# Moving the streamed matmul operands of a four-layer block kernel to one fixed distance from the weights in SBUF

## The chip, the core and the metric

One NeuronCore of a Trainium2 chip runs the whole program in one launch. The metric is the device time of one execution in microseconds. The kernel before takes 1949.94 us (median of 3 runs, 1945.63 to 1951.67).

## What is computed

Two stacked blocks of depth 2 each, in float32, on 256 tokens of width 1024. The first block's layer is a gated MLP, a mixer of three branches (a gated linear recurrence, latent attention, a long depthwise convolution) and a second gated MLP; the second block's layer is an attention mixer and a gated MLP with a short convolution.

```python
def first_block(x, ...):
    for l in range(DEPTH):                       # 2
        x = x + 0.5 * swiglu(rms_norm(x, ffn1_norm[l]), ffn1_w1[l], ffn1_w2[l])
        x = x + hybrid_mixer(rms_norm(x, mix_norm[l]), ...)
        x = x + 0.5 * swiglu(rms_norm(x, ffn2_norm[l]), ffn2_w1[l], ffn2_w2[l])
    return rms_norm(x, final_norm)

def second_block(x, ...):
    for l in range(DEPTH):                       # 2
        x = x + rms_norm_2(hybrid_mixer_2(rms_norm_2(x, attn_pre_norm[l]), ...), attn_post_norm[l])
        x = x + rms_norm_2(conv_ffn(rms_norm_2(x, ffn_pre_norm[l]), ...), ffn_post_norm[l])
    return x
```

The MLPs are 1024 to 2 x 2816 to 1024. Nearly all of the arithmetic is in products of activations with weight matrices that are read once from HBM.

## The kernel before

**One product, three matmuls.** Every weight slab and every activation is held as two `float32r` tiles, a rounded part h and a remainder l. `mm3` (L226 to L229) forms w.x as wh.xh + wh.xl + wl.xh, three matmuls that accumulate in one PSUM bank. In each, a 128 x 128 part of the weights is the stationary operand, which the PE loads with a LDWEIGHTS, and a 128 x 256 slice of the activations (all 256 tokens) is streamed past it. Each matmul thus has a weight load of its own, and the profile shows the loads (engine PEld) beside the matmul of the part before. `tokens3` (L265 to L272) does the same with the roles exchanged: weights are streamed, 256 or 512 columns at a time, past a 128 x 128 part of the activations.

**Slabs.** `Slab` (L186 to L207) brings 128 x 1024 weights (512 KB) by one SyncE DMA (L183) into one of four `raw` tiles; ScalarE copies them to `wh`, VectorE subtracts to `wl` (both L198). A slab feeds 24 matmuls of `mm3`. The tiles rotate through 6 buffers of the pool `w`; in the second block every seventh slab uses a seventh pair of buffers in the pool `w2`, which lies where the first block's scratch was.

**Streamed tiles.** `xh`, `xl` (pool `act`, L508) are the normalised input of every projection; `hh`, `hl` (L591) the hidden layer of the MLPs (pool `ffn`); `r0` to `r3` (pool `mix1`, L694) the branch outputs of the first mixer; `mxh`, `mxl` (pool `mix2`, L1140) the heads' outputs in the second. They are allocated by stack pools in the order in which the program opens them, so each one's address follows from what was opened before it.

**Stages.** Up projections of the MLPs: 11 x 4 groups of 24 matmuls, 1056 in all, with `xh`/`xl` streamed; there are six. Down projections: 528 matmuls with `hh`/`hl` streamed, five times; the sixth and last (L1295) streams the weights 512 wide. The mixers hold the other projections, the attention heads (plain float32 matmuls, L651 to L666) and, on VectorE, a convolution of 31 taps (L916). PE runs in program order; DVE and ACT run the splits of coming slabs and the work behind each projection in the order that the framework fixed. All instruction orders are the same before and after the change.

**Where the tiles lie.** A slab's rows are 512 or 1024 bytes apart, the streamed rows 1024 bytes, so the distance between the start of what is streamed and the start of the weights that are loaded meanwhile, modulo 512 bytes, is one number for each pair of pools. The program's allocation gives, in bytes of a partition modulo 512:

| streamed tile | its start | distance to weights in `w` (start 320) | to weights in `w2` (start 128) |
|---|---|---|---|
| `xh`, `xl` | 320 | 0 | 192 |
| `hh`, `hl` | 128 | 320 | 0 |
| `r0` to `r3` | 160 | 352 | not used together |
| `mxh`, `mxl` | 416 | 96 | 288 |

Where weights are streamed (`tokens3`), the distance is that of the weights to the loaded activations: 0 for `xh`, and 192 (pool `w`) or 0 (pool `w2`) for `hh`. Below, "distance" means this number. SBUF is used to byte 229,152 of 229,376 in each partition, 16,384 of them as scratch for dynamic DMAs.

Of the kernel before, what the change touches and what calls it, by code (L numbers as in the profile page):

```python
# [7 lines left out]
F32 = mybir.dt.float32  # L8
# [8 lines left out]
P = 128  # L17
# [123 lines left out]
def kernel(ctx: ExitStack, tc: tile.TileContext, p, out: bass.AP):  # L141
    nc = tc.nc
# [3 lines left out]
    wpools = [ctx.enter_context(tc.tile_pool(name="w", bufs=6))]  # L146
    act = ctx.enter_context(tc.tile_pool(name="act", bufs=1))
    tmp = ctx.enter_context(tc.tile_pool(name="tmp", bufs=2))
    pso = ctx.enter_context(tc.tile_pool(name="pso", bufs=1, space=PSUM))
    banks = {}  # L150

    @contextmanager
    def psums(n):

        if banks.get('n') == n:
            yield
            return
        with ExitStack() as st:
            banks['n'] = n
            banks['lin'] = st.enter_context(tc.tile_pool(name="psl", bufs=n, space=PSUM, reuse_waits="tile"))  # L160
            if n == 4:
                banks['att'] = st.enter_context(tc.tile_pool(name="psa", bufs=1, space=PSUM, reuse_waits="tile"))
            yield
            banks['n'] = 0
# [439 lines left out]
    def ffn1(w1, w2, cur, nxt, mid=None):  # L604
        with tc.tile_pool(name="ffn", bufs=1, reuse_waits="tile") as fp, psums(7):
            hid = new_hidden(fp)
            a = cur.a
            for jp, pss, r in first_pairs(a, w1, cur.done):
                for i in range(2):
                    j = jp * 2 + i  # L610
                    g = tmp.tile([P, T], F32, name="g")
                    V.tensor_tensor(g, pss[i][:, :T], r, op=ALU.mult)  # L612
                    sg_ = tmp.tile([P, T], F32, name="sg")
                    S.activation(sg_, g, AF.Silu)  # L614
                    u = tmp.tile([P, T], F32, name="u")
                    V.tensor_tensor(u, pss[2 + i][:, :T], r, op=ALU.mult)
                    V.tensor_tensor(u, u, sg_, op=ALU.mult)
                    split(hid.h[:, j, :], hid.l[:, j, :], u)
            if mid is not None:
                mid()  # L620
            project_down(w2, hid, res_add(nxt, 0.5), table=mid is None)
# [66 lines left out]
    def mixer1(l, cur, nxt):  # L688
        a = cur.a
        w = p['w_in'][l]  # L690
        mp = ctx2.enter_context(tc.tile_pool(name="mix1", bufs=1, reuse_waits="tile"))
        fs = [mp.tile([P, n], F32, name=f"f{i}") for i, n in enumerate((1280, 1280, 1036, 1024, 1024, 2048, 0, 1144, 1024)) if n]
        fs.insert(6, fs[5][:, 1024:])
        rs = [mp.tile([P, n], F32R, name=f"r{i}") for i, n in enumerate((1280, 1280, 1024, 1024))]  # L694
        v4 = lambda t_, k=4: t_[:, :k * T].rearrange("p (k n) -> p k n", k=k)
        for par in range(2):
# [254 lines left out]
    def mixer2(l, cur, post):  # L951
        a = cur.a
        w = p['w_in_2'][l]
        mp = ctx2.enter_context(tc.tile_pool(name="mix2", bufs=1, reuse_waits="tile"))
# [180 lines left out]
        for m in range(2):  # L1135
            PE.matmul(ps[:, 0:64], hvr[:, m].rearrange("p j g n -> p (j g n)"), w2s[1][:, m, :], start=m == 0, stop=m == 1)
        V.tensor_tensor(vcz.rearrange("p a i d -> p (a i) d"), ps[:, 0:64].rearrange("p (o d) -> p o d", o=1).to_broadcast([P, 8, 64]),
                        hmask[:, :, None].to_broadcast([P, 8, 64]), op=ALU.mult)

        mix = Act(mp.tile([P, 8, T], F32R, name="mxh"), mp.tile([P, 8, T], F32R, name="mxl"))  # L1140
        os = {}

# [122 lines left out]
    def ffn2(l, cur, post, fp):  # L1265
        hid = new_hidden(fp)
        a = cur.a
        wu = p['w_up_2'][l]
        ups = [fp.tile([P, T + 2], F32, name=f"up{i}") for i in range(4)]
        for u in ups:  # L1270
            G.memset(u[:, 0:2], 0.0)
        n = 0
        for jp, pss, r in first_pairs(a, wu, cur.done):
            for i in range(2):
                j = jp * 2 + i
                cs = []
                for half in range(2):
                    jj = j + KF * half
                    u = ups[n % 4]
                    n += 1  # L1280
                    V.tensor_tensor(u[:, 2:], pss[2 * half + i][:, :T], r, op=ALU.mult)
                    c = tmp.tile([P, T], F32, name="g" if half else "u")
                    S.activation(c, u[:, 0:T], AF.Identity, scale=prm('cw0', l, jj), bias=prm('cb2', l, jj))
                    for q in (1, 2):
                        V.scalar_tensor_tensor(c, u[:, q:q + T], prm('cw%d' % q, l, jj), c, op0=ALU.mult, op1=ALU.add)
                    cs.append(c)
                sg = tmp.tile([P, T], F32, name="sg")
                S.activation(sg, cs[0], AF.Silu)
                V.tensor_tensor(sg, sg, cs[1], op=ALU.mult)
                split(hid.h[:, j, :], hid.l[:, j, :], sg)  # L1290
        if post is None:
            return hid
        project_down(p['w_down_2'][l], hid, post.take)
# [67 lines left out]
    for l in range(2):  # L1361
        cur, nxt = nxt, Next('mix_norm', l)
        ffn1(p['ffn1_w1'][l], p['ffn1_w2'][l], cur, nxt, prep1 if l == 0 else None)
        if l == 0:
            start.close()
        cur, nxt = nxt, Next('ffn2_norm', l)
        with ExitStack() as ctx2:
            ctx2.enter_context(psums(4))
            mixer1(l, cur, nxt)
        cur, nxt = nxt, Next('ffn1_norm', 1) if l == 0 else Joint()  # L1370
        ffn1(p['ffn2_w1'][l], p['ffn2_w2'][l], cur, nxt)
    wpools.append(ctx.enter_context(tc.tile_pool(name="w2", bufs=1)))
    for l in range(2):
        cur = nxt
        with ExitStack() as ctx2:
            pp = ctx2.enter_context(tc.tile_pool(name="post1", bufs=1, reuse_waits="tile"))
            ctx2.enter_context(psums(4))
            post = Post(pp, 'attn_post_norm', l)
            mixer2(l, cur, post)
            nxt = Next('ffn_pre_norm', l)  # L1380
            post.done(nxt)
        cur = nxt
        with ExitStack() as ctx2:
            pp = ctx2.enter_context(tc.tile_pool(name="ffn", bufs=1, reuse_waits="tile"))
            ctx2.enter_context(psums(7))
            if l == 0:
                post = Post(pp, 'ffn_post_norm', l)
                ffn2(l, cur, post, pp)
                nxt = Next('attn_pre_norm', 1)
                post.done(nxt)  # L1390
            else:
                last(l, ffn2(l, cur, None, pp), pp)
# [21 lines left out]
```

## Time and profile before

| | |
|---|---|
| median of 3 runs | 1949.94 us |
| the profiled execution | 1949.49 us |
| its span, first to last instruction | 1947.8 us |
| PE busy | 1921.6 us (99%), 15292 matmuls |
| DVE busy | 1498.5 us (77%) |
| ACT busy | 1122.6 us (58%) |
| granted TensorE clock, mean | 0.997 |
| HBM traffic | 167 GB/s over the span |

The matmuls are pipelined: each is shown with a length of about 0.28 us, but they start about 0.12 us apart, so the pace of PE is read from the starts of successive matmuls (the timeline), not from the mean length of one. "PE busy" is the union of the overlapping lengths and says only that PE has hardly a gap. A row of a timeline gives the start in us from the span's start, the length, and the instruction; a row of stages gives, for each engine, busy time and number of instructions in that stretch.

### The profile page before, as it was taken

What the parts mean: (1) busy time and instruction counts of PE and PEld (TensorE: products, weight loads), DVE (VectorE), ACT (ScalarE), POOL (GpSimd) and SP (SyncE); (2) the same over time, 40 slices, a digit from 0 to 9 for tenths busy, and PEclk for the clock granted to TensorE, in tenths of its full rate; (3) what the DMA queues carried; (4) which work ended last, traced back from release to release, by engine and by line L of the source; (5) the groups of instructions that cost most, each with busy time, mean ns of one, the idle gap of its engine ahead of it and who ended that gap; (6) DMA issues with size and microseconds to landing.
All of it is one profiled execution on the core that took longest, in us unless ns stands there. A gap on an engine that the chain in (4) does not pass through costs nothing.

```text
span 1947.8 us, 38941 instructions
## 1 busy us (share of the span) xinstructions
PE 1921.6 (99%) x15292; PEld 1872.8 (96%) x15292; DVE 1498.5 (77%) x3041; ACT 1122.6 (58%) x1895; POOL 75.5 (4%) x225
## 2 busy tenths in 40 slices
PE   8999999999999999999999999999999999999998
PEld 8999999999999999999999999988999999899997
DVE  7667798896665665699987666877799778769983
ACT  6445677564444544568565445456667545657653
POOL 8000000000000000000000000110000011000000
PEclk9999999999999999999999999999999999999999
DMA  8655545546555555654546555571366547234652
GB/s 252 192 169 186 169 147 154 181 157 193 185 175 191 186 184 171 184 179 132 154 160 198 182 176 183 148 226 47 97 193 208 180 130 219 86 109 152 207 195 86
DMA packets 329879, 327.36 MB, mean 168 GB/s; under 512 B 16956, under 2 KB 323648, under 8 KB 329696
## 3 DMA queue, kind: packets, MB, share of 16 engines
q1 hardware_dynamic: 326336, 322.71, 53.0%
q0 software_dynamic: 3344, 2.16, 0.5%
q8 instruction: 120, 1.97, 0.4%
q14 instruction: 63, 0.52, 0.1%
q10 hardware_dynamic: 16, 0.00, 0.0%
HBM read 323.76 MB, written 1.05 MB: 167 GB/s over the span
## 4 chain that ended last, share of the span: by engine, by line
PE 87%; DVE 8%; ACT 2%; DMA 2%; issue 1%; SPq 0%; DVEq 0%; ACTq 0%
PE lin L227 25%; PE lin L229 25%; PE lin L228 25%; DVE wl L198 3%; PE o L665 2%; PE lin L270 1%; PE lin L272 1%; PE lin L271 1%; PE pt L651 1%; DMA raw<-in_w_in_dram 1%; PE sc L660 1%; DVE f L916 1%; ACT wh L198 1%; PE o L666 1%; PE sc L659 1%
## 5 line engine op out<-in xcount | busy, mean ns | idle before, releaser
L198 DVE TENSOR_TENSOR wl<-raw,wh 128x1024 fp32r<-128x1024 f32 (+2 forms) x644 | 748.7, 1168 | 306.2 <-ACT wh L198 301.7
L198 ACT CAST wh<-raw 128x1024 fp32r<-128x1024 f32 (+2 forms) x644 | 642.7, 1003 | 531.7 <-PE lin L228 371.3
L227 PE MATMUL lin<-xh,wh 128*128 128x256 f32 (+1 forms) x3120 | 884.3, 285 | 2.5 <-ACT xh L504 1.5
L228 PE MATMUL lin<-xl,wh 128*128 128x256 f32 (+1 forms) x3120 | 885.7, 284 | 0.0
L229 PE MATMUL lin<-xh,wl 128*128 128x256 f32 (+1 forms) x3120 | 884.7, 284 | 0.0
L227 PEld LDWEIGHTS lin<-xh,wh 128*128 128x128 f32 (+1 forms) x3120 | 596.6, 192 | 5.6 <-ACT xh L504 2.9
L228 PEld LDWEIGHTS lin<-xl,wh 128*128 128x128 f32 (+1 forms) x3120 | 598.6, 192 | 0.9
L229 PEld LDWEIGHTS lin<-xh,wl 128*128 128x128 f32 (+1 forms) x3120 | 598.1, 192 | 0.7
L227 PE MATMUL lin<-hh,wh 128*128 128x256 f32 x880 | 246.0, 279 | 0.0
L229 PE MATMUL lin<-hh,wl 128*128 128x256 f32 x880 | 245.5, 279 | 0.0
L228 PE MATMUL lin<-hl,wh 128*128 128x256 f32 x880 | 245.3, 279 | 0.0
L229 PEld LDWEIGHTS lin<-hh,wl 128*128 128x128 f32 x880 | 165.4, 188 | 0.0
L227 PEld LDWEIGHTS lin<-hh,wh 128*128 128x128 f32 x880 | 165.2, 188 | 0.0
L228 PEld LDWEIGHTS lin<-hl,wh 128*128 128x128 f32 x880 | 164.9, 187 | 0.0
L227 PE MATMUL lin<-r,wh 128*128 128x256 f32 x372 | 107.9, 290 | 0.5 <-ACT f L870 0.4
L229 PE MATMUL lin<-r,wl 128*128 128x256 f32 x372 | 106.7, 287 | 0.0
L228 PE MATMUL lin<-r,wh 128*128 128x256 f32 x372 | 105.7, 284 | 0.0
L916 DVE SCALAR_TENSOR_TENSOR f<-f,pcol,f 128x256 f32<-128x256 f32 x240 | 103.6, 479 | 0.9
L227 PEld LDWEIGHTS lin<-r,wh 128*128 128x128 f32 x372 | 70.1, 189 | 1.6 <-ACT f L870 0.8
L228 PEld LDWEIGHTS lin<-r,wh 128*128 128x128 f32 x372 | 70.6, 190 | 0.3
L614 ACT ACTIVATE sg<-g 128x256 f32<-128x256 f32 x88 | 35.6, 413 | 60.8 <-DVE g L612 60.7
L229 PEld LDWEIGHTS lin<-r,wl 128*128 128x128 f32 x372 | 69.8, 188 | 0.2
(435 smaller groups left out, 2353.8 us busy)
## 6 DMA issues: line engine op xcount, KB each, us to landing
raw<-in_ffn_w_dram SPq DMA_DIRECT2D x256, 512.0 KB, 3.6
raw<-in_w_in_dram SPq DMA_DIRECT2D x116, 512.0 KB, 3.6
raw<-in_w_up_dram SPq DMA_DIRECT2D x88, 512.0 KB, 4.1
raw<-in_w_down_dram SPq DMA_DIRECT2D x42, 512.0 KB, 3.4
raw<-in_w_out_dram SPq DMA_DIRECT2D x32, 512.0 KB, 3.4
raw<-in_w_in_dram SPq DMA_DIRECT2D x32, 256.0 KB, 3.6
raw<-in_ffn_w_dram SPq DMA_DIRECT2D x16, 256.0 KB, 3.0
raw<-in_lru_w_out_dram SPq DMA_DIRECT2D x8, 512.0 KB, 4.6
```

Source lines behind the costliest of these rows:

```text
L198: i = S.copy(dst(h), src(raw)), V.tensor_tensor(dst(lo), src(raw), f32(dst(h)), op=ALU.subtract)
L227: PE.matmul(ps, wh, xh, start=first, stop=False)
L228: PE.matmul(ps, wh, xl, start=False, stop=False)
L229: PE.matmul(ps, wl, xh, start=False, stop=last)
L270: PE.matmul(ps, xh, wh, start=first and k == 0, stop=False)
L271: PE.matmul(ps, xh, wl, start=False, stop=False)
L272: PE.matmul(ps, xl, wh, start=False, stop=last and k == kt - 1)
L614: S.activation(sg_, g, AF.Silu)
L651: PE.transpose(pt[:, i * P:(i + 1) * P], e[:, i * P:(i + 1) * P], ident)
L659: PE.matmul(sc[:, 0:P], q[:, 0:P], k[:, 0:P], start=True, stop=True)
L665: PE.matmul(o[:, 0:T], v[:, 0, :], pt[:, 0:T], start=first, stop=False)
L916: i = V.scalar_tensor_tensor(cc[:, c, :], pcin[:, c, j:j + T], prm('cdw', l, 4 * j + c), cc[:, c, :], op0=ALU.mult, op1=ALU.add)
```

## The change

Unused tiles ("gaps") are put into the pools so that each streamed tile starts at 256 modulo 512, while all weights' tiles start at 320, those of `w2` included. Every pair that was at distance 0, 96, 192, 288, 320 or 352 is then at 256 - 320, that is 448, modulo 512; where the weights are streamed the distance is 64. The scratch for dynamic DMAs is halved to 8 KB, which makes room for the gaps; SBUF is then used to byte 222,080. No instruction is added, removed or moved on any engine, and no wait differs; only addresses do.

```diff
+    def gap(pool, n, name="gap"):
+        return pool.tile([P, n // 4], F32, name=name, bufs=1)
+
+    gap(act, 448)
+    gap(tmp, 192)
...
@@ mixer1
         fs.insert(6, fs[5][:, 1024:])
+        gap(mp, 480)
         rs = [mp.tile([P, n], F32R, name=f"r{i}") for i, n in enumerate((1280, 1280, 1024, 1024))]
...
@@ mixer2
+        gap(mp, 224)
         mix = Act(mp.tile([P, 8, T], F32R, name="mxh"), mp.tile([P, 8, T], F32R, name="mxl"))
...
     wpools.append(ctx.enter_context(tc.tile_pool(name="w2", bufs=1)))
+    gap(wpools[1], 64)
...
             pp = ctx2.enter_context(tc.tile_pool(name="post1", bufs=1, reuse_waits="tile"))
+            gap(pp, 448)
...
             pp = ctx2.enter_context(tc.tile_pool(name="ffn", bufs=1, reuse_waits="tile"))
+            gap(pp, 448)
...
-    nc = _bacc.Bacc("TRN2", target_bir_lowering=False, num_devices=1)
+    nc = _bacc.Bacc("TRN2", target_bir_lowering=False, num_devices=1, dynamic_dma_scratch_size=8192)
```

## Rows read from the trace of the kernel before

**Rows 1.** The page: busy time of each engine; then the chain that ended last.

```profile
PE 1921.6 (99%) x15292; PEld 1872.8 (96%) x15292; DVE 1498.5 (77%) x3041; ACT 1122.6 (58%) x1895; POOL 75.5 (4%) x225
...
PE 87%; DVE 8%; ACT 2%; DMA 2%; issue 1%; SPq 0%; DVEq 0%; ACTq 0%
```

**Rows 2.** Groups by line and shape: busy us, mean ns of one, idle before.

```profile
L228 PE MATMUL lin<-xl,wh 128*128 128x256 f32 x3088 | 876.8, 284 | 0.0
L229 PEld LDWEIGHTS lin<-xh,wl 128*128 128x128 f32 x3088 | 593.8, 192 | 0.5
L229 PE MATMUL lin<-hh,wl 128*128 128x256 f32 x880 | 245.5, 279 | 0.0
L229 PEld LDWEIGHTS lin<-hh,wl 128*128 128x128 f32 x880 | 165.4, 188 | 0.0
L1100 PEld LDWEIGHTS lin<-wl,winh 128*66 128x66 f32 x64 | 8.7, 136 | 0.0
```

**Rows 3.** Timeline of PE, first up projection: distance 0, first and last of 102.

```profile
59.82 0.28 PE L229 MATMUL lin<-xh,wl 128*128 128x256 f32 x1
...
71.94 0.28 PE L228 MATMUL lin<-xl,wh 128*128 128x256 f32 x1
```

**Rows 4.** Timeline of PE, first down projection: distance 320, first and last of 104.

```profile
159.77 0.28 PE L228 MATMUL lin<-hl,wh 128*128 128x256 f32 x1
...
171.90 0.28 PE L229 MATMUL lin<-hh,wl 128*128 128x256 f32 x1
```

**Rows 5.** Timeline of PE, fifth down projection: distance 320, first and last of 99.

```profile
1543.33 0.28 PE L227 MATMUL lin<-hh,wh 128*128 128x256 f32 x1
...
1554.44 0.28 PE L229 MATMUL lin<-hh,wl 128*128 128x256 f32 x1
```

**Rows 6.** Timeline of PE, branch products of the mixer: distance 352, first and last of 103.

```profile
400.73 0.28 PE L228 MATMUL lin<-r,wh 128*128 128x256 f32 x1
...
412.97 0.28 PE L228 MATMUL lin<-r,wh 128*128 128x256 f32 x1
```

**Rows 7.** Timeline of PE, a slab in `w2`: distance 192, first and last of 27.

```profile
1439.82 0.28 PE L229 MATMUL lin<-xh,wl 128*128 128x256 f32 x1
...
1442.89 0.28 PE L228 MATMUL lin<-xl,wh 128*128 128x256 f32 x1
```

**Rows 8.** Timeline of both: a matmul and the weight load beside it.

```profile
60.06 0.28 PE L228 MATMUL lin<-xl,wh 128*128 128x256 f32 x1
60.06 0.19 PEld L229 LDWEIGHTS lin<-xh,wl 128*128 128x128 f32 x1
```

**Rows 9.** Stages: stretch; PE, PEld, DVE, ACT, POOL busy (count); clock; DMA share; GB/s.

```profile
30.00:140.00 110.00, 110.00 (x919) 110.00 (x919) 78.07 (x122) 55.45 (x83) 19.91 (x39) 1.00 0.63 195
...
226.00:271.00 45.00, 45.00 (x375) 44.95 (x374) 41.57 (x80) 29.85 (x43) 0.00 (x0) 1.00 0.58 176
276.00:298.00 22.00, 22.00 (x186) 22.00 (x185) 21.96 (x41) 17.68 (x32) 1.75 (x3) 1.00 0.32 105
...
339.00:384.50 45.50, 45.50 (x382) 45.50 (x381) 39.69 (x72) 23.17 (x31) 0.00 (x0) 1.00 0.57 174
394.50:434.00 39.50, 39.50 (x332) 39.50 (x331) 35.32 (x71) 27.68 (x46) 0.00 (x0) 1.00 0.53 170
...
1375.50:1392.50 17.00, 17.00 (x143) 16.80 (x142) 11.18 (x19) 9.02 (x14) 0.00 (x0) 1.00 0.50 154
1397.00:1523.00 126.00, 126.00 (x1053) 125.85 (x1052) 122.30 (x239) 89.54 (x146) 0.00 (x0) 1.00 0.58 182
```

**Rows 10.** Timeline of PE, last stage: weights streamed 512 wide past `hh`.

```profile
1899.66 0.39 PE L270 MATMUL lin<-wh,hh 128*128 128x512 f32 x1
...
1900.83 0.39 PE L272 MATMUL lin<-wh,hl 128*128 128x512 f32 x1
```

**Rows 11.** Timeline: POOL's last parameter DMAs, and PE's first work on parameters after that.

```profile
49.86 0.51 POOL L122 DMA_DIRECT2D prow<-in_conv_b_dram  x1
...
140.67 1.05 PE L413 MATMUL lin<-ones,crow 1*128 1x1 f32 x8
```

## The prediction

> **What bounds the kernel now.** I read the page first. PE is busy 99% of the span, with DVE at 77% and ACT at 58%, and the chain that ended last runs through PE for 87% of its length [rows 1]. The reader should not take the 99% for PE at its best: a matmul is shown with 284 ns and its successor starts long before its end [rows 2]. So the second view is the timeline of PE, where the pace is the distance between starts.
>
> In an up projection the first and the last of 102 rows start at 59.82 and 71.94 us: 12.12 us over 101 intervals, **120.0 ns** [rows 3]. In a down projection it is 12.13 us over 103, **117.8 ns** [rows 4]. In the fifth down projection it is 11.11 us over 98, **113.4 ns** [rows 5]. The branch products of the mixer stand at 12.24 us over 102, 120.0 ns again [rows 6], and a slab in `w2` at 3.07 us over 26, 118.1 ns [rows 7]. All five are the same instruction, 128 x 128 weights and 256 columns, without a wait, at a granted clock of 1.00 [rows 9]. What differs is the distance in SBUF: 0, 320, 320, 352 and 192. The weight loads differ as well: 192 ns beside `xl`, 188 beside `hh` [rows 2]. A matmul and the load of the next weights start in the same 10 ns [rows 8]. I read this as the two reads holding each other up, by an amount that depends on where they stand to each other.
>
> The third view is the stages, because a faster PE is worth something only where no other engine takes over. DVE is busy 78 of 110 us in the first up projection, but 122.3 of 126 in the second block's, and 21.96 of 22 in the first mixer's gate stage [rows 9].
>
> **The change, part by part.** It adds, removes and moves no instruction and no wait; on every queue, SP's and POOL's included, the order stands as before. Two things change: the distances, and the DMA scratch.
>
> *The pace at 448.* No row shows this distance for long, so it is bounded by neighbours. Worst steady pace seen: 120.0. Best: 113.4. Two readings place 448 between them. First, by remainders of 128: the distances 320 and 192, which run at 117.8 or 113.4 and 118.1, are both 64 modulo 128, while 0 and 352, at 120.0, are 0 and 96. 448 is 64 modulo 128 too. Second, by where the reads meet. A load of 66 columns takes 136 ns and one of 128 takes 188 [rows 2], so 62 columns cost 52 ns, and 128 columns, 512 bytes, about 107 ns. The stream reads 1024 bytes in some 113 ns, nearly twice as fast, and gains about 512 bytes on the load in the course of one load. If places recur every 512 bytes (my assumption), stream and load meet once per matmul, wherever they start: at distance 0 at the start and again at the end, at 320 after the stream has gained 192 bytes (3/8 of the load), at 448 after 64 bytes, in the first eighth. After that the load is alone. Between 117.8 and 113.4, which distance 320 shows both, I choose **113.4**, since an early meeting leaves most of the load undisturbed; 117.8 is the first rival.
>
> *Block 1's up projections.* Four times 1056 matmuls, less some 60 at the start of the program: 4160 x 6.6 ns = 27.5 us. DVE needs 78 of 110 us there, which at 113.4 would be 104 us long, so nothing takes over.
>
> *Block 2's up projections.* PE would need 1056 x 113.4 = 119.8 us, DVE needs 122.3 [rows 9]. At most 3.7 of the 126 us can go; DVE waits now and then for ACT, so I take 3.0, twice: 6.0 us. What is late next there is the `wl` that DVE makes at L198.
>
> *Down projections.* Four times 528 x (117.8 - 113.4) = 9.3 us. The fifth runs mostly at 113.4 already [rows 5]; I count a third of one of the others, 0.8 us.
>
> *First mixers, two layers.* 226 to 271 us: 375 matmuls x 6.6 = 2.5 us wished for, but DVE needs 41.6 of the 45, so I take 1.8. Gate stage 276 to 298: DVE is full, 0. 339 to 384.5: 382 x 6.6 = 2.5 us. 394.5 to 434: 332 x 6.6 = 2.2 us. That makes 6.5 per layer, 13.0 us.
>
> *Second mixers.* Output projection, 1375.5 to 1392.5: 143 x 6.6 = 0.9 us, twice: 1.9. The rest of all mixers (attention, starts after a stall) is a chain through ACT and DVE, where PE's pace hides behind them: 0 to 3 us, I take 1.5.
>
> *The last stage.* Weights are streamed 512 wide at distance 192, five intervals in 1.17 us, 234 ns each [rows 10]; they go to 64, also 64 modulo 128. I count 0; 264 of them, at a step of 4.4 ns either way, make 1.2 us.
>
> *The scratch of 8 KB.* [...] The parameters' loads are issued by 50 us, and PE first works on prepared parameters at 140.67 us [rows 11]: even at twice the time they are hidden behind 90 us of the first up projection. Cost 0. Without that cover, each us that they came late would be a us of the total.
>
> *The sum.* 27.5 + 6.0 + 9.3 + 0.8 + 13.0 + 1.9 + 1.5 = 60.0 us. The profiled execution took 1949.5 us (span 1947.8), the median of the runs is 1949.9, so the sum is made against a typical one: 1949.5 - 60 = **1889.5 us**, 3.1% faster. Its own range, from the terms bounded by DVE and the mixers, is 1878 to 1903.
>
> [...] The same `float32r` matmul runs at three paces with only its distance changed [rows 3 to 5], and the load beside it is 4 ns longer at distance 0 [rows 2]. [...]
>
> **The rivals.**
>
> 1. *The slower state stays: 117.8 ns at 448.* For it: four of five down projections stay at 117.8 from end to end at distance 320, the same remainder [rows 4]. Then up projections of block 1 gain 4160 x 2.2 = 9.2 us, those of block 2 2 x 2.3 = 4.6, the mixers 2 x 1089 x 2.2 = 4.8 and 1.1 elsewhere, and the fifth down projection loses about 1: 18.7 us, **1931 us**. A mixture of both paces lies between 1889 and 1931.
> 2. *A further step down.* One more step of 4.4 ns, to 109.0, if the two reads no longer meet at all. Up projections of block 1 4160 x 11 = 45.8, of block 2 7 (DVE), down 21.7, first mixers 2 x 10.9, second mixers 5: 101 us, **1848 us**. Against it: no row shows such a pace.
> 3. *Nothing happens,* because the paces come from the stage (PSUM traffic, DVE's writes) and not from the distance: **1949 us**. Against it: the slab in `w2` stands amid a stage at 120.0 and has 118.1 [rows 7].
> 4. *Slower.* 448 belongs with the bad distances. The mechanism is the meeting itself: 64 bytes behind, the stream is stopped in the first eighth of every load, and if it then keeps step with the load instead of passing it, it is held longer than at 0. At 120.0 the `xh` stages stay as they are and the down projections lose 4 x 528 x 2.2 = 4.6 us, the fifth 2.6, the slabs in `w2` 0.6: **1957 us**. At one more step of 2.2 ns, on some 11,400 matmuls, 25 us come on top: 1982. It decides above a pace of about 119.8 ns: there the 7.8 us of loss, less 11,400 x 0.2 ns, pass the 5.8 us that count as slower.
>
> **How the numbers follow.** The forecast has 0.58, rival 1 0.22, rival 2 0.05, rival 3 0.06, rival 4 0.09. The predicted time is the likeliest case, 1889.5 us. The range must hold 8 in 10: the forecast and rival 1 make 0.80, so it reaches from 1868 (the forecast with the terms bounded by DVE better than I think) to 1936 (rival 1 with its mixers gaining nothing). About 0.3% (5.8 us) is what a measurement of this kernel can tell from no change. Faster by more than that: the forecast and rivals 1 and 2, 0.85; within it: rival 3, 0.06; slower: 0.09.
>
> **What would show it.** In the profile after: PE's starts in the first up projection 113.4 ns apart instead of 120.0, the loads beside `xl` at 188 instead of 192 ns; the same 113.4 in all down projections; block 2's up projections at about 123 us with DVE nearly full and PE waiting for `wl`; the gate stage of the first mixers unchanged; the last stage's 234 ns unchanged. The prediction is wrong if the up projections stay at 120.0, if the pace differs between stages that are all at 448, or if PE's pace falls and the stages still keep their lengths.

## The result, and the profile after

| | before | after |
|---|---|---|
| median of the runs, us | 1949.87 | 1895.40 |
| single runs, us | 1945.63 to 1951.67 | 1888.59 to 1906.40 |
| ratio, 95% interval | 1 | 0.973 (0.968 to 0.978) |
| profiled execution, us (span) | 1949.5 (1947.8) | 1888.6 (1886.9) |

The change made the kernel 2.7% faster: 54 us by the medians, 60.8 us between the two profiled executions. The profiled execution of the changed kernel is the shortest of its four runs, and its runs lie 18 us apart where those of before lie 6 apart. The experiments come to what spreads them (E5).

The page, busy time and chain, answering to [rows 1]:

```profile
PE 1857.8 (98%) x15292; PEld 1809.5 (96%) x15292; DVE 1493.8 (79%) x3041; ACT 1121.4 (59%) x1895; POOL 75.7 (4%) x225
...
PE 84%; DVE 9%; ACT 3%; DMA 2%; issue 2%; SPq 0%; DVEq 0%; ACTq 0%
```

The counts of instructions are those of before, and DVE and ACT are busy for nearly the same time; PE alone, with its weight loads, is shorter, and it still makes up most of the chain. The groups by line and shape, answering to [rows 2] (lines have moved by 8: L228 is now L236):

```profile
L237 PEld LDWEIGHTS lin<-xh,wl 128*128 128x128 f32 x3088 | 581.9, 189 | 0.5
L237 PEld LDWEIGHTS lin<-hh,wl 128*128 128x128 f32 x880 | 165.2, 188 | 0.0
...
L236 PE MATMUL lin<-xl,wh 128*128 128x256 f32 x3088 | 860.0, 279 | 0.0
L237 PE MATMUL lin<-hh,wl 128*128 128x256 f32 x880 | 242.9, 276 | 0.0
```

The loads beside `xl` fell from 192 to 189 ns, the matmuls from 284 to 279 and in the down projections from 279 to 276. That 279 is a mean: the timeline of PE in the changed kernel (first and last row of each stretch; start us, length us) shows two paces at one and the same distance. First up projection, 104 rows; first down projection, 109; first mixer, its part that streams `xh` and `xl`, 104; second up projection of block 1, 108; up projection of block 2, 108:

```profile
59.76 0.28 PE L235 MATMUL lin<-xh,wh 128*128 128x256 f32 x1
...
71.89 0.28 PE L236 MATMUL lin<-xl,wh 128*128 128x256 f32 x1
...
149.73 0.28 PE L237 MATMUL lin<-hh,wl 128*128 128x256 f32 x1
...
161.97 0.28 PE L237 MATMUL lin<-hh,wl 128*128 128x256 f32 x1
...
339.82 0.28 PE L236 MATMUL lin<-xl,wh 128*128 128x256 f32 x1
...
351.96 0.28 PE L237 MATMUL lin<-xh,wl 128*128 128x256 f32 x1
...
499.78 0.28 PE L237 MATMUL lin<-xh,wl 128*128 128x256 f32 x1
...
511.91 0.28 PE L236 MATMUL lin<-xl,wh 128*128 128x256 f32 x1
...
1399.79 0.28 PE L237 MATMUL lin<-xh,wl 128*128 128x256 f32 x1
...
1411.92 0.28 PE L236 MATMUL lin<-xl,wh 128*128 128x256 f32 x1
```

In order of time: 12.13 us over 103 intervals, 117.8 ns; 12.24 over 108, **113.3**; 12.14 over 103, **117.9**; 12.13 over 107, 113.4; 12.13 over 107, 113.4. All five are at 448, without a wait and at a granted clock of 1.00. A long run of projections keeps one of the two from its start to its end: the 942 matmuls of the first up projection stand at 117.78 on the mean, the 1582 from the end of the first mixer through the next up and down projections at 113.33.

The stages answering to [rows 9], gate stage of the first mixer and up projection of block 2, each over the same matmuls as there:

```profile
268.06:288.84 20.78, 20.78 (x186) 20.78 (x185) 20.78 (x39) 16.31 (x31) 1.23 (x2) 1.00 0.23 74
...
1350.55:1470.44 119.89, 119.89 (x1053) 119.67 (x1052) 116.08 (x227) 86.09 (x140) 0.00 (x0) 1.00 0.57 179
```

The same 1053 matmuls take 119.9 us that took 126, and PE has no gap in them. DVE, which I had put down for 122.3 us of work there, is busy for 116.1, with 227 instructions where it showed 239; as a share of the stretch that is 97% both times.

### The profile page after: what moved, and what is told of

Read it like the earlier page. It is cut to its first block, busy times and chain, and to the rows that moved or that the text cites. A ratio compares the mean times of both kernels' runs of the same rounds, so it can differ in the third digit from the quotient of the medians.

```text
span 1886.9 us, 38941 instructions
## 1 busy us (share of the span) xinstructions
PE 1857.8 (98%) x15292; PEld 1809.5 (96%) x15292; DVE 1493.8 (79%) x3041; ACT 1121.4 (59%) x1895; POOL 75.7 (4%) x225
## 4 chain that ended last, share of the span: by engine, by line
PE 84%; DVE 9%; ACT 3%; DMA 2%; issue 2%; SPq 0%; DVEq 0%; ACTq 0%
PE lin L235 24%; PE lin L236 24%; PE lin L237 24%; DVE wl L206 3%; DVE f L925 2%; PE o L673 2%; DMA raw<-in_w_in_dram 1%; PE lin L278 1%; PE pt L659 1%; PE lin L280 1%; PE lin L279 1%; PE sc L668 1%; ACT wh L206 1%; PE o L674 1%; PE sc L667 1%
## 5 line engine op out<-in xcount | busy, mean ns | idle before, releaser
L235 PE MATMUL lin<-xh,wh 128*128 128x256 f32 (+1 forms) x3120 | 867.8, 280 | 2.6 <-ACT xh L512 1.5
L236 PE MATMUL lin<-xl,wh 128*128 128x256 f32 (+1 forms) x3120 | 868.8, 279 | 0.0
L237 PE MATMUL lin<-xh,wl 128*128 128x256 f32 (+1 forms) x3120 | 867.6, 279 | 0.0
L235 PEld LDWEIGHTS lin<-xh,wh 128*128 128x128 f32 (+1 forms) x3120 | 584.4, 188 | 6.2 <-ACT xh L512 3.2
L236 PEld LDWEIGHTS lin<-xl,wh 128*128 128x128 f32 (+1 forms) x3120 | 588.9, 189 | 0.9
L237 PEld LDWEIGHTS lin<-xh,wl 128*128 128x128 f32 (+1 forms) x3120 | 586.2, 188 | 0.7
L236 PE MATMUL lin<-hl,wh 128*128 128x256 f32 x880 | 242.9, 276 | 0.0
L236 PEld LDWEIGHTS lin<-hl,wh 128*128 128x128 f32 x880 | 165.2, 188 | 0.0
L236 PE MATMUL lin<-r,wh 128*128 128x256 f32 x372 | 105.5, 284 | 0.0
L236 PEld LDWEIGHTS lin<-r,wh 128*128 128x128 f32 x372 | 70.1, 188 | 0.3
```

Source lines behind the costliest of these rows:

```text
L235: PE.matmul(ps, wh, xh, start=first, stop=False)
L236: PE.matmul(ps, wh, xl, start=False, stop=False)
L237: PE.matmul(ps, wl, xh, start=False, stop=last)
```

## The experiments

**E1, the scratch alone.** The kernel before with

```diff
-    nc = _bacc.Bacc("TRN2", target_bir_lowering=False, num_devices=1)
+    nc = _bacc.Bacc("TRN2", target_bir_lowering=False, num_devices=1, dynamic_dma_scratch_size=8192)
```

> The kernel before with the DMA scratch of 8 KB and no gap. Theory (the addresses decide, the scratch is nothing): 1950 us, within 3 us of before; up projections at 120.0 ns a matmul and the first down projections at 117.8 as before. Rival (part of the gain of 54 us is the scratch): 1940 us or less, with another pace of matmuls although no address of a stream has moved.

Measured: 1949.44 us, ratio 0.9996 (0.9986 to 1.0005). The first up projection stays at 12.12 us over 101 intervals, 120.0 ns. The scratch is worth nothing; the gain is in the gaps.

**E2, all streams at 320.**

```diff
-    gap(act, 448)
+    gap(act, 320)
...
-    gap(wpools[1], 64)
+    gap(wpools[1], 192)
...
-            gap(pp, 448)
+            gap(pp, 320)
```

(the last one twice)

> The change with other gaps, so that every stream of the layers stands 320 bytes past its weights' parts instead of 448; scratch of 8 KB. Theory A (448 is a place of its own; at 320 the matmul keeps to the 117.78 ns of the first four down projections of before): up projections 117.8 ns, no stage at 113.3, and the time about 1930 us. Theory B (only the remainder by 128 counts, 64 at both): the same mixture of 113.33 and 117.78 as at 448 and 1888 to 1906 us. Theory C (both distances allow both states, and which one a stage takes depends on how it was entered): between the two, 1890 to 1930 us, with stages at either pace and others than in the changed kernel.

Measured: 1929.93 us, ratio 0.989 (0.9875 to 0.9908). Timeline of PE, first up projection (104 rows) and first down projection (108 rows):

```profile
59.75 0.28 PE L235 MATMUL lin<-xh,wh 128*128 128x256 f32 x1
...
71.88 0.28 PE L236 MATMUL lin<-xl,wh 128*128 128x256 f32 x1
...
149.83 0.28 PE L235 MATMUL lin<-hh,wh 128*128 128x256 f32 x1
...
161.95 0.28 PE L237 MATMUL lin<-hh,wl 128*128 128x256 f32 x1
```

117.8 ns, and 12.12 us over 107, 113.3. All the up projections and the long runs of 1582, 1534 and 1582 matmuls are at 117.78; the first down projection and a few short runs are at 113.33. So theory A holds for the time (1930), B falls: 320 and 448, both 64 modulo 128, aren't the same place. But 320 too has the faster pace, rarely; theory C holds of it in that.

**E3, all streams at 0.**

```diff
-    gap(act, 448)
...
-    gap(wpools[1], 64)
...
-            gap(pp, 448)
```

(the last one twice)

> The change with the gaps of the streams taken out, so that every stream of the layers stands at distance 0, the down projections and the mixers too; scratch of 8 KB. Theory (distance alone): 120.00 ns in every layer, so the up projections as before, the first four down projections 2.2 ns a matmul slower than before (4 x 528 x 2.2 = 4.7 us), the fifth 6.7 ns (3.5 us), the mixers' projections 0 to 2 us: 1955 to 1962 us. Rival (it is not the distance but the smaller scratch or the shifted tiles as such that pay): under 1940 us.

Measured: 1954.57 us, ratio 1.0029 (1.0015 to 1.0042), 0.4 us under the range that I gave. Timeline of PE, first up projection (103 rows) and first down projection (102 rows):

```profile
59.76 0.28 PE L235 MATMUL lin<-xl,wh 128*128 128x256 f32 x1
...
72.00 0.28 PE L235 MATMUL lin<-xl,wh 128*128 128x256 f32 x1
...
149.82 0.28 PE L236 MATMUL lin<-hh,wl 128*128 128x256 f32 x1
...
161.94 0.28 PE L235 MATMUL lin<-hl,wh 128*128 128x256 f32 x1
```

12.24 us over 102 and 12.12 over 101, both 120.0. Every long run of the layers stands at 120.00, the down projections too, which had been faster at 320. Distance 0 has one pace.

**E4, the matmul streams alone.** Everything else is taken out; a segment is a row of these, behind a short wait for DVE (`o` is the distance in words, `d // 4`):

```python
for s in range(slabs):
    for j, ps in enumerate(pss):
        for i in range(4):
            a = i * 256 + j * P
            b = i * 256 + o
            first, last = s == 0 and i == 0, s == slabs - 1 and i == 3
            PE.matmul(ps[:, :T], wh[:, a:a + P], xh[:, b:b + T], start=first, stop=False)
            PE.matmul(ps[:, :T], wh[:, a:a + P], xl[:, b:b + T], start=False, stop=False)
            PE.matmul(ps[:, :T], wl[:, a:a + P], xh[:, b:b + T], start=False, stop=last)
```

> Leaves out the whole computation: only the three-product matmuls of 256 columns, on fixed weights and streams in SBUF without any other work, at 16 distances of stream from weights (0 to 480 bytes by 32, 240 matmuls each, three times over), and then 20 entries each at 448 and 320. Theory A: 120.0 at 0, 117.8 at 320, 113.3 or 117.8 at 448. Theory B: distances 64, 192, 320 and 448 behave alike and the others are at 120.0. Theory C: at 448 and 320 whole segments stand at either 113.33 or 117.78, by the moment of entry, with no other engine at work. Rival (the two states come from other engines' traffic in the kernel): each distance has one pace here, every time.

Steady pace of each segment of 240 (over its last 60 matmuls), three times each, from the starts in the trace:

```
distance   ns                      distance   ns
   0       120.0 120.0 120.0        256       120.0 120.0 120.0
  32       116.7 116.7 117.8        288       116.7 116.7 117.8
  64       117.8 113.3 117.8        320       117.8 117.8 117.8
  96       120.0 120.0 120.0        352       120.0 120.0 120.0
 128       120.0 118.7 118.7        384       120.0 118.7 118.7
 160       117.3 117.3 117.3        416       118.7 118.7 117.3
 192       113.3 113.3 113.3        448       113.3 113.3 113.3
 224       118.3 118.3 118.3        480       118.3 118.3 118.3
20 entries of 96:  at 448  113.3 in 15, 117.8 in 5;  at 320  117.8 in 20
```

Timeline of PE, three of them: distance 0 (102 rows), 448 (108 rows), and the second entry at 448 among the last 20 (62 rows):

```profile
19.81 0.28 PE L84 MATMUL lin<-xl,wh 128*128 128x256 f32 x1
...
31.93 0.28 PE L83 MATMUL lin<-xh,wh 128*128 128x256 f32 x1
...
434.79 0.28 PE L85 MATMUL lin<-xh,wl 128*128 128x256 f32 x1
...
446.91 0.28 PE L84 MATMUL lin<-xl,wh 128*128 128x256 f32 x1
...
1473.80 0.28 PE L83 MATMUL lin<-xh,wh 128*128 128x256 f32 x1
...
1480.98 0.28 PE L84 MATMUL lin<-xl,wh 128*128 128x256 f32 x1
```

120.0, 113.3 and 117.7 ns (7.18 us over 61). With hardly any work of other engines (DVE is busy for 96.9 us, 5% of the span, ACT not at all, HBM traffic is 2 GB/s) the paces are those of the kernel, so neither PSUM readers nor DVE's or ACT's writes make them, and nor does the weights' DMA. They nearly repeat every 256 bytes: 192 and 448 are the fast places, not 64 and 320; theory B falls for the second time. At 448 one and the same instructions, after one and the same kind of wait, run at either pace: C.

**E5, the changed kernel again.** No edit.

> The changed kernel once more, unaltered. Theory C (at 448 a stage takes 113.33 or 117.78 ns by chance at its entry and keeps it): the profiled execution has other stages in the slower pace than the first one had (there the first up projections, both halves of both mixers), each of its long stages at exactly one of the two, and single times spread over 1880 to 1906 us. Rival (which stage is slow is fixed by what goes before it): the same stages at 117.78 as in the first profile, and times within 6 us, as the kernel before has them.

Measured: 1896.96 us (1892.9 to 1900.6), ratio 0.9725 (0.9706 to 0.9744). Timeline of PE, first up projection (109 rows) and the first up projection of block 2 (105 rows):

```profile
59.73 0.28 PE L236 MATMUL lin<-xl,wh 128*128 128x256 f32 x1
...
71.97 0.28 PE L236 MATMUL lin<-xl,wh 128*128 128x256 f32 x1
...
1399.75 0.28 PE L235 MATMUL lin<-xh,wh 128*128 128x256 f32 x1
...
1412.00 0.28 PE L237 MATMUL lin<-xh,wl 128*128 128x256 f32 x1
```

113.3 and 117.8 ns: just the other way round than in the first profile. The stage from the 132nd to the 1074th matmul takes 106.8 us here and 110.9 there, block 2's up projection 114.7 here and 110.4 there. So the pace of some stages changes from execution to execution, which spreads the times: 4.1 us by this first stage alone. It need not be all of the spread: the longest run of the first set, 1906.40 us, also has the lowest mean granted clock of the four (0.994, the others 0.997), which by 0.003 of 1900 us could be some 6 us (an estimate). The pace of other stages did not change: the 406 matmuls in the second half of each first mixer stood at 117.78 in both profiles, and the runs of 1582, 1534 and 1582 matmuls at 113.33 in both.

**E6, distances close by, and another place of the weights.** E4 with entries of 96 matmuls and a second copy of the weights that begins at 448 modulo 512:

```diff
+        ah, al = (wh2, wl2) if w2 else (wh, wl)
+        d = (d - 128 * w2) % 512
...
-                    PE.matmul(ps[:, :T], wh[:, a:a + P], xh[:, b:b + T], start=first, stop=False)
+                    PE.matmul(ps[:, :T], ah[:, a:a + P], xh[:, b:b + T], start=first, stop=False)
```

> Leaves out the whole computation: matmul streams alone, 13 entries of 96 matmuls in a shuffled order at each of the distances 64, 176, 184, 192, 200, 208, 432, 448, 456 and 464 from weights that begin at 320 modulo 512, and at 192 and 448 from weights that begin at 448 modulo 512. Theory C: 448 gives 113.33 in about three entries of four and 117.78 in the rest, whichever weights; 192, which stood at 113.3 in three entries of three, is either the same lottery (two to four slow entries of 13) or a distance with one state (none of 13). Rival (absolute addresses count as well): the two places of the weights give different paces at the same distance.

```
weights at 320:  64   117.8 in 13        432  119.3 in 13 (119.2 to 119.3)
                176   119.3 in 13        448  113.3 in 13
                184   120.0 in 13        456  120.0 to 120.2 in 13
                192   113.3 in 12,       464  119.1 in 7, 116.7 in 6
                      117.8 in 1
                200   120.0 to 120.2     208  119.1 to 119.3 in 10, 116.7 in 3
weights at 448: 192   113.3 in 4, 117.8 in 9
                448   113.3 in 4, 117.8 in 9
```

The fast place is narrow: at 184 and 200, 8 bytes to either side of 192, and at 456 the pace is 120. And how often each of the two paces comes changes with the second copy of the weights, whether by its place or because the waiting matmul ahead of each entry still loads from the first copy: that was not separated. (By the program's `d - 128` the second copy's two labels stand for each other, 448 where it says 192; both gave the same counts.) 192 is the same lottery as 448.

**E7, all streams at 192.**

```diff
-    gap(act, 448)
+    gap(act, 192)
...
-    gap(wpools[1], 64)
+    gap(wpools[1], 320)
...
-            gap(pp, 448)
+            gap(pp, 192)
```

> The change with every stream at 192 instead of 448. If 192 has the fast state alone: 113.33 ns in all layers, the first up projections 4.6 us (1033 x 4.44 ns) and the mixers' halves 7.3 us (1644 x 4.44 ns) better than in the first profile of the changed kernel, so 1876 to 1884 us and a spread like that of before. If 192 is the same lottery as 448: 1885 to 1906 us with stages at both paces. If the w2 slabs of before (117.7 ns at 192) are the rule for it: about 1930 us.

Measured: 1893.19 us (1887.62 to 1897.31), ratio 0.9707 (0.9687 to 0.9728): as at 448. The 942 matmuls of the first up projection and again all the 406 are at 117.78, the 1582, 1534 and 1582 at 113.33.

**E8, how an entry could be steered.** E4 with ten entries of each kind:

```diff
-        o = d // 4
...
+            oh, ol = (d0 // 4, d0 // 4) if s < 2 and d0 >= 0 else (dh // 4, dl // 4)
```

> Leaves out the whole computation: matmul streams alone, 10 entries of each of 16 kinds in a shuffled order, weights at 320 modulo 512. Nine kinds hold the stream's high part at one distance and its low part (every third matmul) at another; seven run 48 matmuls at another distance (0, 320, 64, 192, 256, 384, 96) and then 72 at 448 without a break. Theory C (a phase that is fixed at entry): after 48 matmuls at 0 or at 256, which have one pace of 120.0, the stream at 448 starts from one phase and takes one state in all ten entries; after 320 or 64, in their 117.78, it stays in the slower state; mixed kinds lie between their parts, and 448 with 192 is at 113.33 or 117.78. Rival (the state is a chance at every change of distance): every kind that ends at 448 shows both states, in about three to one.

Pace at the end of the ten entries:

```
48 matmuls at d, then 448:  d = 0, 256, 384   113.3 in 10, 10, 10
                            d = 192, 96       113.3 in 9, 7
                            d = 320, 64       113.3 in 5, 3
448 throughout                                113.3 in 8
high part at 448, low at 192: 113.3 in 9      high at 192, low at 448: 113.3 in 8
high at 448, low at 320 or 64 (or the reverse): 117.8 in all
high at 448, low at 176: 115.6 in all         high at 448, low at 0: 119.2 to 119.4 in 6, 117.8 in 4
```

A stay at 0, 256 or 384 made 30 entries of 30 fast. Entries at 448 throughout, with the weights at 320, are fast in 39 of 46 over E4, E6 and E8, so that 30 of 30 would come by chance once in a hundred times or less, but ten of ten after 0 alone about once in five: what 0 does by itself is not shown here. 320 and 64 are followed by the slower pace in only 12 of 20, against my expectation. It suggested a better kernel, E11.

**E9, one part undone: the hidden tiles back to 320.**

```diff
-    gap(tmp, 192)
+    gap(tmp, 64)
...
-        gap(mp, 480)
+        gap(mp, 96)
...
-    gap(wpools[1], 64)
+    gap(wpools[1], 192)
```

> The changed kernel with the hidden tiles of block 1 put back to distance 320, where they stood before, and nothing else moved (the gap of the temporaries 64 for 192, those that balance it adapted). My sum (the term of the four down projections, 9.3 us, is one of its own and adds up): downs at 117.8, the rest as in the changed kernel, 1896 + 9.4 = 1905 us, within 5 us for the lottery of the other stages. Rival (the gain is one of the kernel as a whole, and a stage's pace hangs on those beside it): up projections change as well, by more than 10 us in all.

Measured: 1901.45 us, ratio 0.976 (0.9744 to 0.9779). The four down projections take 62.1 us each, as before, and 59.7 to 59.9 in the changed kernel: 9.4 us in all; the up projections of block 1 don't move by it (111.3 to 111.6 us in both profiles). The terms add up. That the median is only 5 to 6 us above that of the changed kernel is within the spread of the other stages.

**E10, how short the stay can be.** E4 at 320 for 24 matmuls and then at 448, with 0 to 12 extra matmuls on shifted weights:

```diff
+                    if s == 2 and i == 0 and j == 0:
+                        for q in range(k):
+                            PE.matmul(dump[:, :T], wh[:, sh:sh + P], xh[:, b:b + T], start=True, stop=True)
```

> Leaves out the whole computation: matmul streams alone, 10 entries of each of 16 kinds, shuffled, weights at 320 modulo 512. Each entry runs 24 matmuls at distance 320 (117.78, the slower state), 24 at 448, then 0, 1, 2, 3, 6 or 12 extra matmuls whose weights are read 64, 192 or 448 bytes further on (distances 384, 256 and 0 for the load beside the stream before them), and then 71 more at 448. Theory C with a fixed phase after 0, 256 and 384: from some number of extra matmuls on, all ten entries end at 113.33, at the latest at 12, as 48 matmuls did it in 30 entries of 30; without extra matmuls, and with three at an unchanged distance, about half end at 117.78. Rival (the kick works by its length, 48 matmuls at 120): even 12 leave two or more of ten at 117.78.

This one tells nothing of its question. The extra matmuls wrote a tile of their own, and as nothing tied them to their place, 624 of the 630 stand at the ends of the first 59 entries, behind the matmuls that they should have steered. What it does show is 24 matmuls at 320 and then 448 without them: 117.8 at the end of 94 entries and 113.3 of 66, where entries at 448 throughout were at 117.8 in 7 of 46. So a stay at 320 makes the slower pace likelier without fixing it. The question needs the order tied down, and was not tried again.

**E11, a stay at distance 0 in the kernel.**

```diff
+KICK = (5, 6, 75, 76, 91, 92, 107, 108, 126, 127, 283, 284, 298, 299, 314, 315, 333, 334, 459, 460, 566, 567)
...
+            o = 112 if fence['all'] in KICK else 0
...
-            h = wpool.tile([P, SL], F32R, name="wh")[:, :kt * n].rearrange("p (k n) -> p k n", k=kt)
+            h = wpool.tile([P, SL + 128], F32R, name="wh")[:, o:o + kt * n].rearrange("p (k n) -> p k n", k=kt)
```

(and the same for `wl`)

> The changed kernel, with the weights of two slabs (48 matmuls) at eleven places, each right behind the wait with which a long run of projections begins, laid 448 bytes further on in their tiles, so that the stream stands at distance 0 from them; all other slabs at 448 as before. If the matmul streams alone are the rule (48 matmuls at 0, then 113.33 in ten entries of ten): all eleven runs go on at 113.33, the two runs of 406 matmuls in the mixers too, which stood at 117.78 in eight cases of eight; cost 11 x 48 x 6.67 ns = 3.5 us, gain about 12 us against the mean of the changed kernel's profiles, so 1885 to 1890 us, and single times closer together. Rival (the phase comes from somewhere else as well, DMA or the conversions of weights): the runs keep a chance of 117.78, and the time stays at 1893 to 1899 us.

Measured: 1928.04 us (1927.02 to 1930.32), ratio 0.989 (0.9866 to 0.9907): 32 us **worse** than the changed kernel. Timeline of PE, first up projection (104 rows), and one of the runs of 1582 matmuls, which has no shifted slab of its own (104 rows):

```profile
59.82 0.28 PE L239 MATMUL lin<-xh,wl 128*128 128x256 f32 x1
...
71.95 0.28 PE L237 MATMUL lin<-xh,wh 128*128 128x256 f32 x1
...
499.81 0.28 PE L238 MATMUL lin<-xl,wh 128*128 128x256 f32 x1
...
511.94 0.28 PE L239 MATMUL lin<-xh,wl 128*128 128x256 f32 x1
```

Both 117.8 ns. Behind all eleven stays the run goes on at 117.78, and the times are within 3.3 us of each other. The stays do not stand right behind the wait, as I had meant, but up to some 60 matmuls after it, and that shows more: three of the runs are at 113.3 until the stay and at 117.8 after it, with no wait between. The last up projection:

```profile
1748.29 0.28 PE L237 MATMUL lin<-xh,wh 128*128 128x256 f32 x1
...
1752.37 0.28 PE L237 MATMUL lin<-xh,wh 128*128 128x256 f32 x1
...
1758.37 0.28 PE L239 MATMUL lin<-xh,wl 128*128 128x256 f32 x1
...
1769.91 0.28 PE L238 MATMUL lin<-xl,wh 128*128 128x256 f32 x1
```

That is 36 intervals at 113.3, 50 at 120.0 (the stay) and 98 at 117.8. The stay does set the pace, but here it sets the slower one. The forecast from the streams alone had the sign wrong.

**E12, the same without the shifts.** Against the changed kernel:

```diff
-            h = wpool.tile([P, SL], F32R, name="wh")[:, :kt * n].rearrange("p (k n) -> p k n", k=kt)
+            h = wpool.tile([P, SL + 128], F32R, name="wh")[:, :kt * n].rearrange("p (k n) -> p k n", k=kt)
```

(and the same for `wl`)

> The run with the shifted slabs without its shifts: the tiles of the weights' parts stay 512 bytes longer, every stream is at 448 as in the changed kernel. Reading 1 (48 matmuls at distance 0, reached by moving the weights, leave the stream at 448 in the slower state, and a run hands its state on to the next): without them the long runs show both paces again and the time is that of the changed kernel, 1890 to 1900 us. Reading 2 (the longer tiles, that is where the weights lie beyond the remainder by 512, decide it): the long runs stay at 117.78, the two of 1582 and 1534 matmuls too, and the time is 1928 less the 3.5 us of the shifted slabs, 1922 to 1928 us.

Measured: 1897.79 us (1889.5 to 1910.65), ratio 0.9736 (0.9703 to 0.9768). The same stretch of the same run, 108 rows:

```profile
499.83 0.28 PE L237 MATMUL lin<-xh,wl 128*128 128x256 f32 x1
...
511.96 0.28 PE L236 MATMUL lin<-xl,wh 128*128 128x256 f32 x1
```

113.4 ns. Reading 1: it was the stay at 0, not where the longer tiles put the weights. (E11 is thus 30 us slower than the same kernel without its stays.) And since the runs of 1582 and 1534 matmuls have no stay of their own, and behind the same short wait went on at 113.33 here and at 117.78 in E11, something of a run outlasts the wait behind it. It is more than the pace: the 406 matmuls ahead of the 1582 are at 117.78 in both. Nor is it so at every wait: in E11 the first down projection stands at 113.3 behind a first up projection at 117.8.

## Why the prediction was right, and where it was off

The time, 1895.4, lies 6 us above the forecast of 1889.5 and inside its range, and that the distance makes it, with nothing else changed, is shown (E1, E3, E4). The sum of 60.0 us met the 60.8 of the profiled execution, but partly by errors that cancel, and by luck: that execution was the shortest of its set, and the profile of E5 gains 52.1. By stages, with the same matmuls at both ends:

| term | forecast, us | measured, us | the same kernel again (E5), us |
|---|---|---|---|
| block 1's up projections, with the start | 27.5 | 23.1 | 26.9 |
| block 2's up projections | 6.0 | 12.3 | 3.7 |
| four down projections | 9.3 | 9.4 | 9.3 |
| fifth | 0.8 | 1.1 | -1.3 |
| first mixers | 13.0 | 11.1 | 10.7 |
| second mixers | 3.4 | 2.9 | 1.9 |
| last stage | 0 | 1.0 | 0.8 |

**The choice of 113.4.** Right as a number for most stages, wrong in both its reasons. By remainders of 128, 320 and 64 would have been as good as 448; they are at 117.8 in nearly every entry, and only 192 and 448 are mostly fast (E4, E6). By the place where the reads meet, 192 would have met after 320 bytes, far into the load, and it is as fast as 448; so that picture falls too, as far as it ordered the distances.

**"113.4 or 117.8", as forecast and rival.** I took them for alternatives of which one would be true. Both are, at the same distance, stage by stage. The rows had shown it: [rows 4] and [rows 5] are both at 320, so that the sentence on three paces "with only its distance changed" did not fit them. The first up projection gained 2.1 us of its 6.5, the mixers' halves behind the gate stage 0.9 each of 2.2 to 2.5; the other three up projections of block 1 gained 6.5 to 7.0 of their 7.0 each. This is the step that failed: "the pace differs between stages that are all at 448" stood among the things that would make the prediction wrong, and it came. The text had a mixture between 1889 and 1931 in its range; 1895 is near the fast end since the longest runs fell there.

**Block 2, "DVE needs 122.3".** Mis-sized: 6.1 us each at 113.3, where I allowed 3.0 (in E5 these stages stand at 117.8 and gain 1.8 each). The same 936 matmuls by the groups of DVE, before (in 111.9 us) and after (in 106.0 us):

```profile
L198 DVE TENSOR_TENSOR wl<-raw,wh 128x1024 fp32r<-128x1024 f32 (+1 forms) x43 | 51.9, 1206 | 0.0
...
L503 DVE TENSOR_TENSOR hl<-sg,hh 128x256 fp32r<-128x256 f32 x20 | 8.4, 419 | 1.5 <-ACT hh L503 1.5
```

```profile
L206 DVE TENSOR_TENSOR wl<-raw,wh 128x1024 fp32r<-128x1024 f32 x41 | 49.9, 1217 | 0.0
...
L511 DVE TENSOR_TENSOR hl<-sg,hh 128x256 fp32r<-128x256 f32 x18 | 7.5, 419 | 1.7 <-ACT hh L511 1.6
```

DVE did not get faster. It did less within the stage: two fewer slabs in these groups and two fewer hidden tiles, at much the same durations. The page has 3041 instructions of DVE both times, so what is missing here lies outside the stage. And 936 matmuls use 39 slabs, at 24 each: DVE prepared 43 before and still 41 after, so its busy time was not what the stage needed. My reading is that a busy share near 97% limits a stage only when its lead in prepared weights and its arrears in results are used up, and that this stage doesn't use them up for 6 us; no run took the lead away to test it. The gate stage of the first mixers, to which I gave 0 for the same reason, gained 1.3 us in each layer.

**The scratch, counted as 0.** Which DMAs it serves no run shows. With the smaller scratch alone (E1) the time is 1949.44 us, ratio 0.9996, and POOL, which issues the parameters' loads, is busy for 20.09 us between 30 and 140 us, 19.91 before [rows 9].

**Mixers.** The attention part gained nothing (-0.2 us per layer), as argued: PE's pace hides there. The halves behind it are short by the slower pace, not by another engine. The second mixers' 2.9 is met by chance: their output projections gained 0.8 each (forecast 0.9), but the rest gained 2.0 in one layer and lost 0.8 in the other, and in E1, where no stream had moved, the second of them lost 4.2.

**The last stage.** At distance 64 its 512-wide matmuls stand at 229 ns (timeline of PE, nine rows), 234 before [rows 10]:

```profile
1841.95 0.39 PE L278 MATMUL lin<-wh,hh 128*128 128x512 f32 x1
...
1843.78 0.39 PE L280 MATMUL lin<-wh,hl 128*128 128x512 f32 x1
```

That is the 1.0 us where I counted 0, inside the 1.2 that I gave as its bound.

**Rivals.** 1 (117.8 stays) is what E2 measures, forecast 1931, measured 1929.9. 4 (slower) is what distance 0 for everything gives, forecast 1957, measured 1954.6. 3 falls with E2 to E4, where the pace goes with the distance and nothing else; 2 shows nowhere: no distance, alone or in the kernel, was held below 113.3.

**What stays open.** What fixes the pace at a run's start. The streams alone take 113.3 after a stay at distance 0 that is made by moving the stream; the kernel takes 117.8 after one that is made by moving the weights. Moving the weights does not decide it alone: in the kernel before, the first slab in `w2` of the fifth down projection is 24 matmuls at 0, with the stream where it stays at 320 for the slabs in `w`, and it leads from the slower pace to the faster:

```profile
1534.04 0.28 PE L229 MATMUL lin<-hh,wl 128*128 128x256 f32 x1
...
1539.81 0.28 PE L227 MATMUL lin<-hh,wh 128*128 128x256 f32 x1
...
1542.09 0.28 PE L228 MATMUL lin<-hl,wh 128*128 128x256 f32 x1
```

That is 49 intervals at 117.8 and 19 at 120.0; [rows 5] follows at 113.4. The profile of E1 has the same, so here too it is the stay, and not the execution, that sets the pace, and the 113.4 on which the forecast rested is the pace behind such stays. Whether the distance that follows, the way in which the stay is made or the place of the weights decides, was not tried. Nor was a stay at 0 made by moving the stream in the kernel. If it made every run fast, it could be worth 13 to 20 us less its own cost, 3.5 us in E11 (an estimate): some 2900 matmuls in the first profile of the changed kernel and some 4500 in E5 stand at 117.78, 4.4 ns above the faster pace. No version here beats the changed kernel beyond the spread of its runs; that at 192 is equal to it.

## What to carry to other kernels

Where PE is the bound and weights are loaded under a running matmul, the place of the stream relative to the weights is worth up to 6% of a matmul here (120.0 against 113.3 ns); measure it with the bare stream at several distances, in steps as small as 8 bytes, and several entries of each, before choosing. Read the pace from the starts of matmuls in each stage apart, and profile the winner twice: a mean over stages or a single profile hides that one distance can have two paces. And before a busy engine is taken for a stage's bound, count how many of its instructions the stage itself needs: what it prepares for its neighbours is in the share too (here 43 slabs, where the stage used 39). Stages before and after are compared over the same matmuls, not over windows of about the same time.

## What the runs showed that I had not expected

- One distance, two steady paces: 113.33 and 117.78 ns at 448 and 192 (and, less often the faster, at 64 and 320), kept for up to 1582 matmuls without a switch, chosen anew behind a wait or a run at another distance. Sets of runs of the kernel spread by up to 21 us (E12), those of the kernel before by 6 to 9.
- The fast place is narrow: 120.0 at 184, 200 and 456, 113.3 at 192 and 448 (E6).
- 48 matmuls at distance 0 set the pace of what follows in the kernel: 117.8 in 11 of 11 (E11), 30 us above the same kernel without them (E12). In the streams alone it is 113.3 in 10 of 10, where 39 of 46 without them are.
